# Seven block products in two more chunks of the first layer, and the last gate's conditioning beside a later stage

## The chip, the cores and the metric

One core of one Trainium2 chip runs the whole program. The metric is the device time of one execution in microseconds (us). The kernel before takes 2086.13 us, the median of three runs (2085.07 to 2087.54).

## The reference, cut to what matters

Two layers over 1024 prompt frames and 32 sample frames of width 1024. Each layer has a mixer and a channel MLP; the conditioning vector `mod` gives shifts, scales and gates. The change touches the MLP's second product and the conditioning.

```python
for i in range(DEPTH):                       # DEPTH = 2
    mod = silu(c) @ w_ada[i] + b_ada[i]      # w_ada[i]: 1024 x 6144
    sh1, sc1, gt1, sh2, sc2, gt2 = split(mod, 6)
    h = rmsnorm(x, g_norm[i, 0]) * (1 + sc1) + sh1
    mix = spatial gating MLP (layer 0) or pooling mixer (layer 1) of h
    x = x + gt1 * rmsnorm(mix, g_norm[i, 1])
    h = rmsnorm(x, g_norm[i, 2]) * (1 + sc2) + sh2
    f = square(relu(h @ ffn_w_up[i])) @ ffn_w_down[i]    # 1024 -> 4096 -> 1024
    x = x + gt2 * rmsnorm(f, g_norm[i, 3])
```

## The kernel before, in words

Activations lie transposed, channels on partitions and frames along the free axis, in three tiles: tiles 0 and 1 have 384 frames each (the pair), tile 2 has 256 prompt frames and the 32 sample frames. Every large product is made of three matmuls, because each operand is split into a high and a low part (`wh`, `wl` for weights, `hh`, `hl` or `fh`, `fl` for activations): wh·h, wh·l, wl·h. The high part is a copy by ScalarE, the low part a subtraction by VectorE.

The MLP runs in chunks of 512 of the 4096 hidden channels, in the order of the list `passes`: chunk 0 for tile 0 and for tile 1 alone, then chunks 1 to 7 for the pair (pair chunks), then four double chunks (0, 2, 4, 6) for tile 2 (the third-tile stage). A chunk has up products (`pf`, `pfa`, `pfb`, `pfc`) into PSUM, the squared ReLU, and down products (`pg`, or `psa`, `psb`, `psc`), which VectorE adds into the accumulator `acc`. In all pair chunks the up product of the two tiles by two halves of the contraction is a 2x2 block product done with seven block multiplications instead of eight (sums of blocks are made once, in `combos`). The down product does the same only in the chunks of the tuple `SEVEN`: there `sevens` makes weight sums for four parts A1, S31, S24, A22, `keep_seven` makes sums of the hidden blocks, and `down_seven` runs the products of `PLAN`. A plain down product of a pair chunk has 192 matmuls, one with seven block products 168. A chunk in `SEVEN` needs three more buffers, `far`, taken from the space of the third tile's accumulator, so whatever that tile still has to do must be finished first.

All weights and conditioning columns come in one list, `stream`, in program order, as loads of 512 KB into a ring of three buffers (`RAW_SLOTS = 3`, tile `raw`). A buffer is free again when ScalarE and VectorE have read it. Weights then go to ten to sixteen split buffers. A conditioning item (`wide`, tile `aa`) is 256 rows by 512 columns of `w_ada`: VectorE multiplies and adds it for both conditioning vectors, and after four items transposes, reduces and folds the sums. `some_ada(n)` puts n items at the current place of the stream; `w_chunk(n, ada)` puts one behind each up pair and each down weight until `ada` are used. The list `rest` ends with the eight items of the second layer's last gate (gt2 of layer 1).

While products are recorded, `weave` interleaves stream steps and `fillers` (norms, residuals, outputs) by a cost model of TensorE and VectorE; a scheduler then fixes one order per engine. SyncE issues nearly all loads and stores in its order. `to_out` is the filler that adds the last residual of tiles 0 and 1, transposes and stores the output; it calls `need_ada(1, 5)`, the last gate. `mix_to_ffn` prepares the third tile's input of the MLP; its last step waits in `late_norm` until the pair chunks are nearly through (`apply` in layer 0; in layer 1 a scaled copy goes to DRAM, and `shift` reads it back).

## Time and profile before

| | us |
|---|---|
| median of three runs | 2086.13 |
| profiled execution, its own time | 2085.84 |
| its span, first to last instruction | 2084.1 |
| TensorE busy | 2062.3 |
| VectorE busy | 1711.5 |
| ScalarE busy | 1114.4 |
| layer 0, pair chunk 5 / 6 / 7, start to start | 62.80 / 63.10 / 62.58 |
| layer 1, pair chunk 4 / 5 / 6 / 7 | 58.85 / 59.40 / 59.41 / 59.54 |
| layer 1, third tile, first / second double chunk | 53.77 / 51.01 |

A chunk is measured from its first up product to the next chunk's first up product, as the timeline of TensorE shows them. Busy time of an engine is the union of its instructions; matmuls overlap each other, so the time that one takes on the way is read from the distance of two starts and not from its length. An idle time is put down to the instruction whose semaphore came last.

### The profile page before, as it was taken

What the parts mean: (1) busy time and instruction counts of PE and PEld (TensorE: products, weight loads), DVE (VectorE), ACT (ScalarE), POOL (GpSimd) and SP (SyncE); (2) the same over time, 40 slices, a digit from 0 to 9 for tenths busy, and PEclk for the clock granted to TensorE, in tenths of its full rate; (3) what the DMA queues carried; (4) which work ended last, traced back from release to release, by engine and by line L of the source; (5) the groups of instructions that cost most, each with busy time, mean ns of one, the idle gap of its engine ahead of it and who ended that gap; (6) DMA issues with size and microseconds to landing.
All of it is one profiled execution on the core that took longest, in us unless ns stands there. A gap on an engine that the chain in (4) does not pass through costs nothing.

```text
span 2084.1 us, 33060 instructions
## 1 busy us (share of the span) xinstructions
PE 2062.3 (99%) x12646; PEld 1988.7 (95%) x12646; DVE 1711.5 (82%) x3149; ACT 1114.4 (53%) x2038; POOL 22.4 (1%) x44
## 2 busy tenths in 40 slices
PE   8999999999999999999999999999999999999998
PEld 5878999999999999999999999999999999999998
DVE  6799777889789998887877989897969688899644
ACT  5633543454247643344436766766445566685555
POOL 0000000000000000000000000000000000000200
PEclk9999999999999999999999999999999999999999
DMA  8585543366444343434334768553233222247873
GB/s 298 154 271 187 173 125 120 120 195 192 141 122 155 107 142 112 132 113 133 114 98 124 214 190 247 166 161 104 89 112 111 75 80 71 69 146 223 210 184 98
DMA packets 411923, 306.27 MB, mean 147 GB/s; under 512 B 47054, under 2 KB 375030, under 8 KB 411636
## 3 DMA queue, kind: packets, MB, share of 16 engines
q1 hardware_dynamic: 410836, 302.88, 47.5%
q8 instruction: 99, 1.62, 0.3%
q0 software_dynamic: 896, 1.28, 0.2%
q14 instruction: 60, 0.49, 0.1%
q10 hardware_dynamic: 32, 0.01, 0.0%
HBM read 272.27 MB, written 31.84 MB: 146 GB/s over the span
## 4 chain that ended last, share of the span: by engine, by line
PE 86%; DVE 7%; ACT 4%; DMA 2%; issue 1%; SPq 0%; DVEq 0%; ACTq 0%
PE pg L1174 9%; PE pg L1175 9%; PE pg L1176 9%; PE pf L1174 4%; PE pf L1176 4%; PE pf L1175 4%; PE pv L1200 2%; PE pv L1202 2%; PE pv L1201 2%; PE pfa L1852 2%; PE pfa L1854 2%; PE pfa L1853 2%; PE po L1174 2%; PE po L1175 2%; PE po L1176 2%; PE pu L1174 2%
## 5 line engine op out<-in xcount | busy, mean ns | idle before, releaser
L1174 PE MATMUL pg<-fh,wh_dn 128*128 128x384 f32 (+1 forms) x800 | 257.9, 323 | 1.4 <-ACT fh L1494 1.0
L1175 PE MATMUL pg<-fl,wh_dn 128*128 128x384 f32 (+1 forms) x800 | 256.7, 321 | 0.0
L1176 PE MATMUL pg<-fh,wl_dn 128*128 128x384 f32 (+1 forms) x800 | 256.4, 321 | 0.3 <-DVE wl_dn L80 0.3
L80 DVE SCALAR_TENSOR_TENSOR aa<-raw,csil,aa 128x512 f32<-128x512 f32 (+1 forms) x364 | 208.7, 623 | 8.3 <-DMA raw<-in_w_ada_dram 8.0
L1174 PE MATMUL pf<-hh,wh_up 128*128 128x288 f32 (+1 forms) x632 | 192.3, 304 | 0.0
L1175 PE MATMUL pf<-hl,wh_up 128*128 128x288 f32 (+1 forms) x632 | 191.1, 302 | 0.0
L1176 PE MATMUL pf<-hh,wl_up 128*128 128x288 f32 (+1 forms) x632 | 190.8, 302 | 0.0
L80 DVE TENSOR_TENSOR wl_dn<-raw,wh_dn 128x1024 fp32r<-128x1024 f32 x120 | 146.3, 1220 | 43.7 <-ACT wh_dn L629 31.4
L80 DVE TENSOR_TENSOR acc<-acc,pg 128x384 f32<-128x384 f32 (+1 forms) x208 | 108.7, 527 | 72.3 <-PE pg L1176 71.4
L629 ACT ACTIVATE wh_dn<-raw 128x1024 fp32r<-128x1024 f32 x120 | 126.9, 1058 | 71.1 <-PE pf L1175 31.3
L1174 PEld LDWEIGHTS pg<-fh,wh_dn 128*128 128x128 f32 x800 | 150.1, 188 | 2.9 <-ACT fh L1494 1.7
L1175 PEld LDWEIGHTS pg<-fl,wh_dn 128*128 128x128 f32 x800 | 150.2, 188 | 0.7 <-DVE fl L80 0.3
L1176 PEld LDWEIGHTS pg<-fh,wl_dn 128*128 128x128 f32 x800 | 150.1, 188 | 0.6 <-DVE wl_dn L80 0.6
L629 ACT ACTIVATE wh_up<-raw 128x1024 fp32r<-128x1024 f32 x79 | 83.6, 1058 | 74.9 <-PE pg L1175 43.8
L1176 PEld LDWEIGHTS pf<-hh,wl_up 128*128 128x128 f32 x632 | 118.9, 188 | 0.3 <-DVE wl_up L80 0.3
L1175 PEld LDWEIGHTS pf<-hl,wh_up 128*128 128x128 f32 x632 | 118.6, 188 | 0.5
L1174 PEld LDWEIGHTS pf<-hh,wh_up 128*128 128x128 f32 x632 | 118.4, 187 | 0.6 <-ACT wh_up L629 0.2
L80 DVE TENSOR_TENSOR wl_up<-raw,wh_up 128x1024 fp32r<-128x1024 f32 x79 | 96.2, 1220 | 18.7 <-ACT wh_up L629 18.7
L1174 PE MATMUL pg<-fx,wh_dn 128*128 128x288 f32 (+1 forms) x320 | 98.7, 309 | 0.1
L1175 PE MATMUL pg<-fx,wh_dn 128*128 128x288 f32 (+1 forms) x320 | 97.5, 305 | 0.0
L1176 PE MATMUL pg<-fx,wl_dn 128*128 128x288 f32 (+1 forms) x320 | 97.3, 304 | 0.0
L80 DVE TENSOR_TENSOR wl_up_S<-raw,wh_up_S 128x512 fp32r<-128x512 f32 (+1 forms) x84 | 71.6, 865 | 28.4 <-PE pfb L1853 16.2
(932 smaller groups left out, 6108.4 us busy)
## 6 DMA issues: line engine op xcount, KB each, us to landing
raw<-in_ffn_w_up_dram SPq DMA_DIRECT2D x136, 512.0 KB, 4.0
raw<-in_ffn_w_down_dram SPq DMA_DIRECT2D x136, 512.0 KB, 3.8
raw<-in_w_ada_dram SPq DMA_DIRECT2D x90, 512.0 KB, 4.1
raw<-in_sgu_w_in_dram SPq DMA_DIRECT2D x48, 512.0 KB, 4.3
raw<-in_sgu_w_out_dram SPq DMA_DIRECT2D x32, 512.0 KB, 3.6
xd<-acc SPq DMA_DIRECT2D x8, 1536.0 KB, 8.2
xo_r<-xd SPq DMA_DIRECT2D x32, 384.0 KB, 4.1
vd<-vt SPq DMA_DIRECT2D x32, 256.0 KB, 3.7
```

Of the source, the lines that this page charges most:

```text
L80: return op(out, *args, **kw)
L629: act(out=wh, in_=r, func=AF.Copy)
L1174: mm(ps[:, :n], wh, rh, start=i == 0, stop=False)
L1175: mm(ps[:, :n], wh, rl, start=False, stop=False)
L1176: mm(ps[:, :n], wl, rh, start=False, stop=i == last)
L1200: mm(ps[:m, :], a_h, wh[:, o : o + 512], start=k == 0, stop=False)
L1201: mm(ps[:m, :], a_h, wl[:, o : o + 512], start=False, stop=False)
L1202: mm(ps[:m, :], a_l, wh[:, o : o + 512], start=False, stop=k == KB - 1)
L1852: mm(ps[:, :n], wh[:, o], rh, start=first and k == 0, stop=False, skip_group_check=True)
L1853: mm(ps[:, :n], wh[:, o], rl, start=False, stop=False, skip_group_check=True)
L1854: mm(ps[:, :n], wl[:, o], rh, start=False, stop=k == HK - 1, skip_group_check=True)
```

## The change

Layer 0's pair chunks 5 and 6 join `SEVEN`. So that the third tile's accumulator is free for `far` there, layer 0's third tile takes the path that only layer 1 had: eight channel blocks are scaled in place, stored to a DRAM tile `scaled`, and read back by `shift`. In layer 1 the same copy now goes to `scaled` and not to `xd[2]`. Conditioning items move: layer 0's pair chunks had 5, 6, 6, 6, 6, 6, 1 (chunks 1 to 7) and now have 5, 7, 8, 8, 0, 0, 4; layer 1's pair chunks had the last four and now have none; the last gate's eight items stand in the first double chunk of layer 1's third tile. Within a chunk they are spread evenly over its calls. `to_out` waits until the stream has passed them. At the start of every down product with seven blocks, the first half of a third product is moved ahead.

```diff
+    scaled = dram.tile([P, KB, ncol[-1]], F32, name="scaled")
...
-        left = [ada]
+        at = [0]
         def one_ada():
-            if left[0] > 0:
-                left[0] -= 1
-                some_ada(1)
+            i, calls = at[0], 6 * m
+            at[0] += 1
+            some_ada((i + 1) * ada // calls - i * ada // calls)
...
-    SEVEN = ((1, 4), (1, 5), (1, 6), (1, 7))
+    SEVEN = ((0, 5), (0, 6), (1, 4), (1, 5), (1, 6), (1, 7))
...
-            w_chunk(n, (1 if c < 3 else 2) if l else (5 if c == 1 else 6) if c < 7 else 1)
+            w_chunk(n, 0 if l else {1: 5, 2: 7, 3: 8, 4: 8, 5: 0, 6: 0, 7: 4}[c])
             continue
-        w_chunk(n)
+        w_chunk(n, 8 if l and c == 0 and tiles == [NT - 1] else 0)
...
-            for i in (1, 5):
+            for i in (1, 5, 2):
                 product(0, i, (0,))
-            for i in (1, 5):
+            for i in (1, 5, 2):
                 product(0, i, (1,))
                 behind(0, i)
-            for i in (2, 6, 3, 7):
+            for i in (6, 3, 7):
                 run(0, i)
...
-            if l == 0:
-                late_norm.append((f"ffn{l}_{t}", apply(t, l, 2, 3, got[0])))
-                return
             for k in range(KB):                 # scale acc in place
...
-            nc.sync.dma_start(xd[t], acc[t][:, :, HALO:])
+            nc.sync.dma_start(scaled, acc[t][:, :, HALO:])
             late_norm.append((f"ffn{l}_{t}", shift(t, l)))
...
-        nc.sync.dma_start(hl[t].bitcast(F32), xd[t])
+        nc.sync.dma_start(hl[t].bitcast(F32), scaled)
...
+            while state["next"] <= max(ada_last[(1, 20 + i)] for i in range(4)):
+                yield 1.0
             need_ada(1, 5)
```

Three places of the built programs show the moves. First TensorE at the start of the down product of layer 0's chunk 5. In the names, `pg_5_0_0` is the accumulation of chunk 5, tile 0, first output block; `psa`, `psb`, `psc` are the three banks of the seven products, `fh` and `fl` hidden blocks split into high and low, B and T plain blocks and sums, `wh_dn_0_A` a weight part. Before:

```order
L1174 MATMUL pg_5_0_0_9905<-fh_5_0_0_9655,wh_dn_0_9766 128x384
L1175 MATMUL pg_5_0_0_9905<-fl_5_0_0_9656,wh_dn_0_9766 128x384
L1176 MATMUL pg_5_0_0_9905<-fh_5_0_0_9655,wl_dn_0_9767 128x384
L1174 MATMUL pg_5_0_0_9905<-fh_5_0_1_9685,wh_dn_0_9766 128x384
L1175 MATMUL pg_5_0_0_9905<-fl_5_0_1_9686,wh_dn_0_9766 128x384
```

The same place now:

```order
L1984 MATMUL psa_5_0_9963<-fh_5_B_0_9762,wh_dn_0_A_9796 128x384
L1985 MATMUL psa_5_0_9963<-fl_5_B_0_9763,wh_dn_0_A_9796 128x384
L1986 MATMUL psa_5_0_9963<-fh_5_B_0_9762,wh_dn_0_A_9796 128x384
L1984 MATMUL psb_5_0_9967<-fh_5_T_0_9767,wh_dn_0_S_9817 128x384
L1985 MATMUL psb_5_0_9967<-fl_5_T_0_9768,wh_dn_0_S_9817 128x384
L1986 MATMUL psb_5_0_9967<-fh_5_T_0_9767,wh_dn_0_S_9817 128x384
L1984 MATMUL psc_5_0_9971<-combo_R,wh_dn_0_A_9796 128x384
L1985 MATMUL psc_5_0_9971<-combo_R,wh_dn_0_A_9796 128x384
L1986 MATMUL psc_5_0_9971<-combo_R,wh_dn_0_A_9796 128x384
L1984 MATMUL psa_5_0_9963<-fx_5_B_1_9922,wh_dn_0_A_9796 128x384
L1985 MATMUL psa_5_0_9963<-fx_5_B_1_9922,wh_dn_0_A_9796 128x384
```

Seven products replace the plain ones, and the nine first matmuls use blocks of the first half; the late block `fx_5_B_1` comes tenth. Next VectorE in the first double chunk of layer 1's third tile, behind the last sums of the pair. `wl_up_4` is the low part of its fifth up weight, `aa_10` a conditioning sum, `acc_66` and `acc_67` are the accumulators of tiles 0 and 1, `sq_rf` their squares. Before:

```order
L80 TENSOR_TENSOR acc_66<-acc_66,da_7_3_19267 128x384
L80 TENSOR_TENSOR wl_up_4_19303<-raw_19173,wh_up_4_19302 128x1024
L80 TENSOR_TENSOR fl_0_2_0_19298<-r_0_2_0_19295,fh_0_2_0_19297 128x288
L80 TENSOR_TENSOR acc_67<-acc_67,psa_7_3_19184 128x384
L80 TENSOR_TENSOR wl_up_5_19316<-raw_19229,wh_up_5_19315 128x1024
L80 TENSOR_TENSOR sq_rf_0_19360<-sq_rf_0_19360 128x384
```

The same place now:

```order
L80 TENSOR_TENSOR acc_66<-acc_66,da_7_3_19360 128x384
L80 TENSOR_SCALAR aa_10_512_0_19363<-raw_19266,csil 128x512
L80 TENSOR_SCALAR aa_10_512_1_19364<-raw_19266,csil 128x512
L80 SCALAR_TENSOR_TENSOR aa_10_512_0_19363<-raw_19266,csil,aa_10_512_0_19363 128x512
L80 SCALAR_TENSOR_TENSOR aa_10_512_1_19364<-raw_19266,csil,aa_10_512_1_19364 128x512
L80 TENSOR_TENSOR fl_0_2_0_19399<-r_0_2_0_19396,fh_0_2_0_19398 128x288
L80 TENSOR_TENSOR wl_up_4_19404<-raw_19322,wh_up_4_19403 128x1024
L80 TENSOR_TENSOR acc_67<-acc_67,psa_7_3_19277 128x384
L80 TENSOR_TENSOR wl_up_5_19450<-raw_19352,wh_up_5_19449 128x1024
```

The conditioning stands in VectorE's row between the weights. From this sum up to and with the low part of the next double chunk's first weight, the row gains 40 instructions on `aa`, its transposes and reductions and one `xlast` transpose, and loses 14 of the output residual of tile 0. Last SyncE, some loads later in the same stage; before:

```order
L533 DMA raw_19409<-in_ffn_w_down_dram 128x8x128
L533 DMA raw_19454<-in_ffn_w_down_dram 128x8x128
L533 DMA raw_19503<-in_ffn_w_down_dram 128x8x128
L2086 DMA xraw<-xtd 32x32x32 x2
L533 DMA raw_19549<-in_ffn_w_down_dram 128x8x128
```

The same place now:

```order
L534 DMA raw_19673<-in_ffn_w_down_dram 128x8x128
L534 DMA raw_19716<-in_ffn_w_down_dram 128x8x128
L2087 DMA xraw<-xtd 32x32x32
L534 DMA raw_19778<-in_w_ada_dram 128x2x512
L534 DMA raw_19784<-in_ffn_w_down_dram 128x8x128
L534 DMA raw_19816<-in_w_ada_dram 128x2x512
L2087 DMA xraw<-xtd 32x32x32
```

Eight conditioning loads share the three `raw` buffers with the stage's sixteen weight loads. (`xraw` is the residual of the third tile for the end.)

## The prediction, as put on record before the change was run

> **What bounds the kernel now.** I read the page's busy shares first, then its chain of waits, then the windows chunk by chunk, then single rows of the timeline where a term needed them.
>
> ```profile
> span 2084.1 us, 33060 instructions
> PE 2062.3 (99%) x12646; PEld 1988.7 (95%) x12646; DVE 1711.5 (82%) x3149; ACT 1114.4 (53%) x2038; POOL 22.4 (1%) x44
> PE 86%; DVE 7%; ACT 4%; DMA 2%; issue 1%; SPq 0%; DVEq 0%; ACTq 0%
> ```
>
> TensorE is busy 99% of the span, and the chain runs over it for 86%. So a matmul less is a gain, and anything else counts only where it makes TensorE wait. The profiled execution took 2085.84 us: its span and 1.7 around it. The median of the runs is 0.3 higher; I sum against the former and add 0.3 at the end.
>
> Now the stages that the change touches, as windows between first up products. Columns: length, TensorE, its weight loads, VectorE, ScalarE, GpSimd, clock, DMA.
>
> ```profile
> core 0: us, PE busy (x) PEld busy (x) DVE busy (x) ACT busy (x) POOL busy (x), PEclk, DMA share, GB/s
> 757.06:820.55 63.49, 63.13 (x372) 62.78 (x372) 57.86 (x104) 26.86 (x48) 0.00 (x0) 1.00 0.38 117
> 820.55:883.45 62.90, 62.90 (x370) 62.62 (x369) 51.51 (x85) 26.94 (x47) 0.00 (x0) 1.00 0.37 118
> 883.45:945.85 62.40, 62.40 (x361) 62.40 (x361) 53.18 (x87) 24.93 (x45) 0.00 (x0) 1.00 0.38 119
> 945.85:1008.65 62.80, 62.80 (x369) 62.52 (x369) 50.34 (x81) 27.05 (x47) 0.00 (x0) 1.00 0.37 118
> 1008.65:1071.75 63.10, 62.97 (x370) 62.61 (x369) 52.69 (x87) 25.06 (x45) 0.00 (x0) 1.00 0.37 117
> 1071.75:1134.33 62.58, 62.58 (x361) 62.36 (x361) 43.30 (x77) 38.11 (x77) 0.00 (x0) 1.00 0.32 97
> 1628.61:1687.46 58.85, 58.48 (x332) 57.08 (x331) 49.47 (x97) 36.40 (x76) 0.00 (x0) 1.00 0.18 55
> 1687.46:1746.86 59.40, 59.25 (x338) 58.19 (x337) 52.78 (x103) 39.32 (x80) 0.00 (x0) 1.00 0.23 71
> 1865.81:1919.58 53.77, 53.42 (x395) 52.67 (x395) 50.19 (x81) 33.91 (x60) 1.28 (x2) 1.00 0.79 225
> 1919.58:1970.59 51.01, 51.01 (x387) 50.91 (x385) 37.01 (x54) 26.78 (x41) 13.61 (x22) 1.00 0.85 220
> ```
>
> The first six rows are layer 0's pair chunks 2 to 7 with the plain down product, the next two are layer 1's chunks 4 and 5 with seven block products, the last two are the first double chunks of layer 1's third tile. Everywhere TensorE has the full clock and almost no gap. VectorE has 5 to 20 us free in a pair chunk, but in the first double chunk of the third tile only 53.77 − 50.19 = 3.6.
>
> **Seven products in layer 0's chunks 5 and 6.** Each drops 24 of its 192 down matmuls. The trap is the matmul's length:
>
> ```profile
> 799.57 0.33 PE L1176 MATMUL pg<-combo_R,wl_dn 128*128 128x384 f32 x1
> 799.75 0.33 PE L1174 MATMUL pg<-fh,wh_dn 128*128 128x384 f32 x1
> 799.92 0.33 PE L1175 MATMUL pg<-fl,wh_dn 128*128 128x384 f32 x1
> 787.27:820.55 33.28, 33.28 (x192) 33.12 (x192) 8.21 (x15) 0.00 (x0) 1.00 0.44 132
> ```
>
> Each is listed at 0.33 us, but the next starts 0.17 later, and the last row, the window of one whole down product for its tile alone, gives 33.28 / 192 = 0.1733 us. So 48 matmuls are 8.3 us and not 15.8. The Trainium skill, "TensorE: Matmul & The Clock Gate", section "Wait — 56ns, not 53.3ns?", has a warm start-to-start of columns / 2.4 GHz + about 2.5 ns, an estimate of 0.1625 us for 384 columns; by it the 48 would save 7.8, and the trace's own 0.1733 decides.
>
> Not all of 8.3 arrives, since block sums and waits come with it. The windows say what does: chunks 5 and 6 take 62.80 + 63.10 = 125.90 now, and layer 1's chunks 4 and 5, the same two steps in the same order (first seven chunk, then one behind another), take 58.85 + 59.40 = 118.25. That is 7.65 less. But the last product of a seven chunk leaves its last six matmuls for the next chunk, so 6 × 0.1733 = 1.04 falls into chunk 7. **−6.6**. Ends: −8.3, no overhead at all; −6.0, if the first seven chunk also runs at 59.40. VectorE's 49.47 and 52.78 there hold norms that layer 0 has not at this place, and conditioning is moved out of both chunks, so nothing on VectorE should be fuller than in the template.
>
> **The third product's early half.** Seven down products now number six, and each opens with three more matmuls that need only first-half blocks.
>
> ```profile
> 1718.49 0.34 PE L1985 MATMUL psb<-fh_T,wh_dn_S 128*128 128x384 f32 x1
> 1718.98 0.44 PE L1983 MATMUL psa<-fx_B,wh_dn_A 128*128 128x384 f32 x1 [0.15 <-ACT fx_B L1494]
> 1719.42 0.55 DVE L80 TENSOR_TENSOR fx_B<-r,fx_B 128x384 fp32r<-128x384 f32 x1
> 1720.06 0.41 PE L1984 MATMUL psa<-fx_B,wh_dn_A 128*128 128x384 f32 x1
> ```
>
> Chunk 5 of layer 1: TensorE gets to the late block at 1718.98, waits for its high part, then for its low part, which VectorE ends at 1719.97; the next matmul is at 1720.06. Three matmuls (0.52) put in between push the block's first use back by about as much as they fill, and what follows starts about 0.1 earlier (1720.92 for 1721.01, by adding starts). 6 × 0.1 = **−0.6**; ends 0 and −3.0 (all of 0.5 each).
>
> **Conditioning in layer 0's chunks 1 to 4.** Chunks 2, 3, 4 get one, two and two more items, chunk 7 three more; the third tile's scaling (16 instructions) moves out of chunk 7 into this region, together with a store and a reload on SyncE's queue. The price of an item:
>
> ```profile
> 820.52 0.88 DVE L80 TENSOR_SCALAR aa<-raw,csil 128x512 f32<-128x512 f32 x2 [1.30 <-DMA raw<-in_w_ada_dram]
> 821.32 1.41 DVE L80 SCALAR_TENSOR_TENSOR aa<-raw,csil,aa 128x512 f32<-128x512 f32 x2
> 822.65 0.55 DVE L80 TENSOR_TENSOR acc<-acc,pg 128x384 f32<-128x384 f32 x1
> L80 DVE STREAM_TRANSPOSE raw<-aa 128x512 f32<-128x512 f32 x28 | 18.7, 692 | 0.0
> L733 DVE TENSOR_REDUCE part<-raw 128x16 f32<-128x512 f32 x28 | 18.1, 666 | 0.0
> ```
>
> Two multiply-adds take 1.33 from start to next start (0.665 each), two plain multiplies 0.80; each fold of four items has two transposes and two reductions, 18.7 / 28 = 0.67 and 18.1 / 28 = 0.65. An item is four passes, 2.66, and a quarter of a fold, some 3.1 us with its wait. Five items are 15.5, and 16 scalings at about 0.28 are 4.5 (estimate, from the 0.55 of a 384-column pass). Free in chunks 2 to 4 are 5.6, 11.4 and 9.2 us: 26.2 for 20. It fits, but the same row of VectorE also serves the sums that TensorE waits for, and chunk 2, the fullest of the three, shows 0.36 us of TensorE idle (63.49 − 63.13). Two such gaps: **+0.7**; ends 0 and +3 (one item's length, if one sum is late by a whole item). Chunk 7's three items, 9.3, lie in 62.58 − 43.30 = 19.3 free: 0. Cover gone, they would cost up to their length. The store and reload lie before chunk 5 in a queue at 0.38 DMA share: 0, unless `shift` is late for chunk 7's end, which is four chunks later.
>
> **Layer 1's chunks without items.** Four items leave chunks that had VectorE time free: **−0.2** (0 to −1).
>
> **The last gate in the third tile's first double chunk.** Here is the price. VectorE's row there, in rows from now:
>
> ```profile
> 1870.36 0.55 DVE L80 TENSOR_TENSOR acc<-acc,da 128x384 f32<-128x384 f32 x1
> 1885.26 0.40 PE L1176 MATMUL pg<-fh,wl_dn 128*128 128x288 f32 x1 [0.32 <-DVE wl_dn L80]
> 1890.10 1.23 DVE L80 TENSOR_TENSOR wl_dn<-raw,wh_dn 128x1024 fp32r<-128x1024 f32 x1 [1.41 <-ACT wh_dn L629]
> 1908.36 1.22 DVE L80 TENSOR_TENSOR wl_up<-raw,wh_up 128x1024 fp32r<-128x1024 f32 x1
> 1919.85 0.29 PE L1176 MATMUL pf<-hh,wl_up 128*128 128x288 f32 x1
> L80 DVE SCALAR_TENSOR_TENSOR acc<-acc,coef,r_rf 128x384 f32<-128x384 f32 x16 | 9.3, 610 | 0.0
> L80 DVE TENSOR_TENSOR acc<-acc,xo_r 128x768 f32<-128x768 f32 x8 | 7.6, 951 | 0.0
> L80 DVE STREAM_TRANSPOSE xlast<-xraw 128x1024 f32<-128x1024 f32 (+1 forms) x3 | 3.7, 1241 | 0.0
> ```
>
> Between the sum at 1870.36 and the next double chunk's first low part (1908.36, ready 1909.6, used first by the matmul at 1919.85) the row gains 28 × 0.665 + 4 × 0.40 + 4 × 0.67 + 4 × 0.65 = 25.5 and one transpose of 1.24, and loses 14 residual passes: 8 × 0.58, 3 × 0.95, 3 × 0.55 = 9.1. Net 17.6. The row is fixed, so the low part moves from 1909.6 to 1927.2, or to 1923.6 if all 3.6 of idle are filled. TensorE wants it at 1919.85: it waits 3.8 at least (3.0 if some of the passes overlap as starts do), 7.4 if no idle is filled.
>
> The loads can add to this. Sixteen weights and eight items share three buffers, where there were sixteen loads.
>
> ```profile
> raw<-in_ffn_w_up_dram SPq DMA_DIRECT2D x10, 512.0 KB, 4.7
> raw<-in_ffn_w_down_dram SPq DMA_DIRECT2D x8, 512.0 KB, 4.5
> raw<-in_w_ada_dram SPq DMA_DIRECT2D x90, 512.0 KB, 4.1
> L629 ACT ACTIVATE wh_up<-raw 128x1024 fp32r<-128x1024 f32 x9 | 9.5, 1057 | 8.4 <-PE pg L1175 7.2 <-DMA raw<-in_ffn_w_up_dram 1.2
> ```
>
> The first two are medians in this window, the third of the whole run. A buffer's turn is the landing, 4.6, and ScalarE's copy 1.06 and VectorE's subtraction 1.22, 6.9 us; for an item 4.1 and 2.66, 6.8. Twenty-four loads on three buffers are eight turns, 55 us if no turn waits for anything, as long as the stage. That reader passes queue behind each other's rows is sure, since VectorE would be full; with a wait of 1 us a turn, 63, which is 9.5 over 53.77. By slot and item, the twelve loads from the down weights to the next up weights run four turns of about 7.4, 30 us, where TensorE asks for eight weights at 3.2 (51.01 / 16), 25.6: 4 more. Part of that is the same delay as VectorE's. I take **+6** between +3.0 and +9.5, nearer to the row of VectorE, of which I am surer. The bytes themselves: 225 GB/s at a share of 0.79 make 285 at a full share; the stage's 12.1 MB and 4.2 more are 57.2 us by that, no more than VectorE's own floor.
>
> The Trainium skill, "DMA: Bandwidth & Descriptors", section "Anatomy of one DMA — SWDGE (gpsimd) path", gives a transfer 2.0 us and bytes / 436 GB/s, an estimate of 3.2 us for 512 KB. By it turns would be over 1 us shorter, VectorE alone would set the stage and the sum would be some 2 us lower. It is stated for GpSimd's path, and the rows of SyncE's queue, 4.1 to 4.7, disagree.
>
> Queued behind the items on SyncE are weights and `xraw`; behind them on VectorE the low parts, so TensorE. The residual and the stores of tiles 0 and 1 move later by about 50 us:
>
> ```profile
> L2489 SPq DMA_DIRECT2D out_dram<-y_sq x40: 316/562/1537, 1919.3 to 1999.2; - x40
> ```
>
> They would end near 2050, some 30 us before the span's end, and their passes fit the 14 us that VectorE has free in the second double chunk: 0.
>
> Sum: −6.6 − 0.6 + 0.7 − 0.2 + 6 = −0.7, own time 2085.1, with the 0.3 **2085.4**.
>
> **Rivals.** *The third tile's loss is small, faster.* If buffers turn in the shadow of VectorE and VectorE's passes overlap, the stage loses 3.0; with 0.3 in chunks 2 to 4 and 0.2 for each reordered start: −6.6 − 1.2 − 0.2 + 0.3 + 3.0 = −4.7, 2081.4. For it: the slack of 10 us between 1909.6 and 1919.85, in which a late low part hurts nobody. Against it: TensorE already waits 0.32 at 1885.26, in the middle of the stage, where no such slack exists.
>
> *The ring bounds the stage, slower.* If every one of eight turns waits 1.35 (about VectorE's one idle of 1.41 for a copy, or one low part ahead), the stage takes 8 × 8.25 = 66, +12.2; with −6.7 elsewhere, +5.5: 2091.6. It decides from a loss of 10.9 in the stage on. For it: DMA share 0.79 and landings longer here than elsewhere. Against it: loads run ahead of the stage, and the pair chunks before it leave the ring idle most of the time.
>
> *Seven chunks save less in layer 0 than in layer 1*, because chunk 4's eight items reach into chunk 5, where VectorE makes 24 hidden sums: both chunks at about 60.9 instead of 59.1 lose some 3 us: 2088.4. Against it: nothing of conditioning is due in chunks 5 and 6.
>
> **How the numbers follow.** Differences under 0.2% (4.2 us) can't be told from none, so faster is below 2082.0 and slower above 2090.3. Forecast 0.42, small loss 0.30, ring 0.18, dearer seven chunks 0.10, of which 0.06 within the bound. Faster 0.30, same 0.48, slower 0.22. The range goes from 2079.5 (small loss with the early halves at −3) to 2091.5 (the ring's case), leaving out about one in ten on each side.
>
> **What would show it.** Right: chunks 5 and 6 of layer 0 at about 58.9 and 59.4; chunks 2 to 4 each within 0.7 of now; the third tile's first double chunk at 57 to 63, TensorE waiting there for `wl_dn` and `wl_up`, VectorE for `raw`; last stores of tiles 0 and 1 before 2060. Wrong: that stage under 56 or over 64, a seven chunk over 60.5, or waits that move into the second double chunk, where the residual's passes would then stand in the way.

## The result: 2108.05 us, 1.0% slower

The changed kernel takes 2108.05 us, the median of four runs (2105.77 to 2110.45), against 2086.05 for the kernel before on the same chip; the ratio is 1.0105, with a 95% interval of 1.0087 to 1.0122. The forecast was 2085.4, in a range of 2079.5 to 2091.5. The profiled execution took 2109.03, its span 2107.2.

From the page of the changed kernel, the lines that answer to those shown of before, and the group of the conditioning sums:

```profile
span 2107.2 us, 33152 instructions
PE 2063.9 (98%) x12598; PEld 1984.4 (94%) x12598; DVE 1749.4 (83%) x3247; ACT 1139.9 (54%) x2106; POOL 22.4 (1%) x44
PE 77%; DVE 11%; DMA 5%; ACT 5%; issue 2%; DVEq 0%; ACTq 0%; SPq 0%
L80 DVE SCALAR_TENSOR_TENSOR aa<-raw,csil,aa 128x512 f32<-128x512 f32 (+1 forms) x364 | 206.8, 621 | 16.6 <-DMA raw<-in_w_ada_dram 16.4
```

TensorE has 48 matmuls less and 23 us more span. The chain of waits tells where: TensorE's share fell from 86% to 77%, VectorE's rose from 7% to 11% and that of the transfers from 2% to 5%. VectorE waits 16.4 us in front of conditioning sums for their loads, 8.0 before, with the same number of sums.

Windows of the changed kernel, columns as before: layer 0's chunks 3, 4, 5, 6; its chunk 7 together with the third tile's first double chunk; layer 1's chunk 7 together with the third tile's first double chunk; the second double chunk. Chunk 7 and what follows are taken together because a few matmuls of the third tile now run ahead inside chunk 7.

```profile
core 0: us, PE busy (x) PEld busy (x) DVE busy (x) ACT busy (x) POOL busy (x), PEclk, DMA share, GB/s
819.03:885.64 66.61, 64.48 (x369) 62.42 (x369) 57.31 (x95) 25.68 (x46) 0.00 (x0) 1.00 0.40 126
885.64:952.19 66.55, 64.56 (x370) 62.32 (x370) 56.14 (x90) 25.67 (x46) 0.00 (x0) 1.00 0.41 128
952.19:1010.49 58.30, 57.85 (x331) 57.18 (x331) 50.25 (x98) 38.10 (x78) 0.00 (x0) 1.00 0.24 72
1010.49:1069.87 59.38, 58.88 (x337) 58.24 (x337) 52.76 (x103) 39.36 (x80) 0.00 (x0) 1.00 0.23 71
1069.87:1191.59 121.72, 118.79 (x765) 117.19 (x765) 106.64 (x176) 80.91 (x150) 0.00 (x0) 0.99 0.58 176
1813.22:1935.39 122.17, 114.88 (x728) 111.84 (x727) 108.91 (x195) 78.55 (x161) 0.00 (x0) 0.99 0.54 159
1935.39:1992.15 56.76, 54.68 (x397) 53.42 (x398) 48.26 (x77) 29.11 (x47) 4.36 (x7) 0.97 0.75 210
```

The same two joined stages before:

```profile
1071.75:1186.50 114.75, 114.75 (x751) 114.32 (x751) 92.05 (x149) 78.52 (x147) 0.00 (x0) 1.00 0.49 147
1806.27:1919.58 113.31, 112.81 (x731) 110.89 (x731) 103.30 (x190) 82.49 (x167) 1.28 (x2) 1.00 0.56 164
```

By start-to-start distances the whole difference is laid out:

| stage | before | changed | difference | forecast |
|---|---|---|---|---|
| up to layer 0's chunk 2 | 757.06 | 755.17 | −1.9 | 0 |
| layer 0, chunks 2, 3, 4 | 188.8 | 197.0 | +8.2 | +0.7 |
| layer 0, chunks 5, 6 | 125.9 | 117.7 | −8.2 | −7.6, less starts |
| layer 0, chunk 7 and third tile's first double chunk | 114.8 | 121.7 | +7.0 | +1.0 |
| rest of layer 0's third tile, layer 1 up to its pair chunks | 228.5 | 231.4 | +2.9 | 0 |
| layer 1, chunks 1 to 6 | 391.3 | 390.2 | −1.1 | −0.2, less starts |
| layer 1, chunk 7 and third tile's first double chunk | 113.3 | 122.2 | +8.9 | +6 |
| layer 1, third tile, the rest to the last matmul | 157.5 | 164.9 | +7.4 | 0 |

The gain came as forecast. Four stages gave back 31.5 us, nearly four times as much. In the rows that were read, TensorE waits there for a split weight or a hidden block that comes late from VectorE or ScalarE; its two longest waits in the third tile's first double chunk of layer 1 are these (us in total, times, longest):

```profile
PE pg L1177 <- DVE wl_dn L80: 3.5, 3, 2.1
PE pg L1175 <- ACT wh_dn L630: 2.6, 2, 1.4
```

Of the −1.9 ahead of chunk 2, 1.1 lies in chunk 1, whose five items stand one call later than before: 78.2 for 79.3. Place matters in this direction too.

### The profile page after: what moved, and what is told of

It reads as the page before. It is cut to its first block, busy times and chain, and to the rows that moved or that the text cites. A ratio compares the mean times of both kernels' runs of the same rounds, so it can differ in the third digit from the quotient of the medians.

```text
span 2107.2 us, 33152 instructions
## 1 busy us (share of the span) xinstructions
PE 2063.9 (98%) x12598; PEld 1984.4 (94%) x12598; DVE 1749.4 (83%) x3247; ACT 1139.9 (54%) x2106; POOL 22.4 (1%) x44
## 4 chain that ended last, share of the span: by engine, by line
PE 77%; DVE 11%; DMA 5%; ACT 5%; issue 2%; DVEq 0%; ACTq 0%; SPq 0%
PE pg L1175 7%; PE pg L1176 7%; PE pg L1177 7%; PE pf L1177 3%; PE pf L1175 3%; PE pf L1176 3%; PE pv L1201 2%; PE pv L1203 2%; PE pv L1202 2%; PE pfa L1853 2%; PE pfa L1855 2%; PE pfa L1854 2%; DMA raw<-in_w_ada_dram 2%; PE po L1176 2%; PE po L1175 2%
## 5 line engine op out<-in xcount | busy, mean ns | idle before, releaser
L1175 PE MATMUL pg<-fh,wh_dn 128*128 128x384 f32 (+1 forms) x720 | 231.8, 322 | 4.4 <-ACT wh_dn L630 2.6
L1177 PE MATMUL pg<-fh,wl_dn 128*128 128x384 f32 (+1 forms) x720 | 230.5, 320 | 3.6 <-DVE wl_dn L80 3.5
L1176 PE MATMUL pg<-fl,wh_dn 128*128 128x384 f32 (+1 forms) x720 | 230.6, 320 | 2.4 <-DVE fl L80 2.4
L80 DVE SCALAR_TENSOR_TENSOR aa<-raw,csil,aa 128x512 f32<-128x512 f32 (+1 forms) x364 | 206.8, 621 | 16.6 <-DMA raw<-in_w_ada_dram 16.4
L80 DVE TENSOR_TENSOR wl_dn<-raw,wh_dn 128x1024 fp32r<-128x1024 f32 x112 | 136.2, 1219 | 28.8 <-ACT wh_dn L630 19.9
L630 ACT ACTIVATE wh_dn<-raw 128x1024 fp32r<-128x1024 f32 x112 | 118.2, 1057 | 71.9 <-DMA raw<-in_ffn_w_down_dram 41.8
L1175 PEld LDWEIGHTS pg<-fh,wh_dn 128*128 128x128 f32 x720 | 135.5, 188 | 6.8 <-ACT wh_dn L630 3.4
L1177 PEld LDWEIGHTS pg<-fh,wl_dn 128*128 128x128 f32 x720 | 135.5, 188 | 4.5 <-DVE wl_dn L80 4.5
L1176 PEld LDWEIGHTS pg<-fl,wh_dn 128*128 128x128 f32 x720 | 135.6, 188 | 3.1 <-DVE fl L80 2.9
L80 DVE TENSOR_TENSOR acc<-acc,pg 128x384 f32<-128x384 f32 (+1 forms) x176 | 91.5, 522 | 50.3 <-PE pg L1177 49.6
L1175 PE MATMUL pg<-fx,wh_dn 128*128 128x288 f32 (+1 forms) x304 | 93.3, 308 | 1.6 <-ACT fx L1495 1.6
L1176 PE MATMUL pg<-fx,wh_dn 128*128 128x288 f32 (+1 forms) x304 | 91.9, 303 | 0.0
```

Source lines behind the costliest of these rows:

```text
L80: return op(out, *args, **kw)
L630: act(out=wh, in_=r, func=AF.Copy)
L1175: mm(ps[:, :n], wh, rh, start=i == 0, stop=False)
L1176: mm(ps[:, :n], wh, rl, start=False, stop=False)
L1177: mm(ps[:, :n], wl, rh, start=False, stop=i == last)
```

## The experiments

Most edits change only where conditioning items stand and which chunks are in `SEVEN`. `w_chunk` gets the number of items for each of its six calls in a pair chunk (behind two up pairs, then four down weights) as a list:

```diff
-            some_ada((i + 1) * ada // calls - i * ada // calls)
+            some_ada(ada[i] if ada else 0)
```

A reader needs the changed kernel's lists: chunk 2 has 1,1,1,1,1,2, chunks 3 and 4 have 1,1,2,1,1,2, chunk 7 has 0,1,1,0,1,1, and the third tile's double chunk 0,1,1,0,1,1,0,1,1,0,1,1. "Joined" means chunk 7 with the double chunk behind it. The kernel before, measured beside the experiments, took 2086.57 us (e1 to e4), 2087.61 (e5 to e8), 2088.24 (e9 to e13, one run) and 2087.64 (e14, e15), and each total below is to be held against its own.

**e1: the last gate's items in layer 1's pair chunks.**

```diff
-(1, 1), (1, 2), (1, 3): no items; third tile: 8
+(1, 1): [0,0,1,0,0,1], (1, 2): [0,1,0,1,0,1], (1, 3): [0,1,0,1,0,1]; third tile: none
```

> The changed kernel with one thing moved: the last gate's eight items stand in layer 1's pair chunks 1, 2, 3 (two, three, three) and not in the third tile's first double chunk. Theory P (the items in the third-tile stage are the price there: 62.40 and 56.70 us in the first two double chunks for 53.77 and 51.01 before, and 2 at the end): those windows go back to within 1 us of before, a gain of 14 to 16; layer 1's chunks 1 to 3 show 10 to 20 us of free VectorE time each and lose 0 to 3; time about 2094 (2092 to 2097). Rival Q (an item costs what it costs wherever it stands, since VectorE is late everywhere in pair chunks too): chunks 1 to 3 of layer 1 grow by some 1 us an item, 8 together; time about 2100.

Measured: 2109.07 us, ratio 1.0110 (1.0093 to 1.0127), no better than the change.

```profile
1572.48:1644.63 72.15, 67.79 (x388) 66.03 (x388) 56.98 (x106) 33.66 (x62) 0.00 (x0) 0.99 0.37 108
1644.63:1709.62 64.99, 62.09 (x333) 59.47 (x333) 50.75 (x110) 37.08 (x78) 0.00 (x0) 0.96 0.25 76
1829.02:1942.50 113.48, 112.44 (x731) 110.92 (x731) 103.63 (x190) 82.37 (x167) 1.28 (x2) 1.00 0.56 164
1942.50:1993.51 51.01, 51.01 (x387) 50.91 (x385) 36.57 (x54) 26.78 (x41) 13.57 (x22) 1.00 0.84 218
```

The last two rows are back at 113.3 and 51.0, so the first half of theory P is shown. But chunks 3 and 4 of layer 1 (first two rows) went from 62.95 and 58.54 to 72.15 and 64.99. Some 14 us moved along with the items (chunks 1 to 6 together). With 15 us of VectorE free in the 72.15 window, that is not plain lack of time. Part of it is this: the first seven block chunk (4) takes the third tile's accumulator, so that tile's norm must be finished by then, and TensorE stood 3.7 us for it just ahead of chunk 4. Rival Q had the direction, and 8 was too little.

**e2: the items' loads without most of their passes.**

```diff
+                if l == 1 and sl >= 10 and (c, v) != (0, 0) and not (q == 0 and c == 0):
+                    continue
```

> The changed kernel, but the last gate's eight items keep all eight loads and their places in the ring, and leave out 22 of their 32 VectorE passes (so the last gate is not computed fully). Theory V (VectorE's row is the bound of the third tile's first double chunk): 22 x 0.665 = 14.6 us less on VectorE, the window goes from 62.40 to 54 to 56. Rival R (the ring of three buffers with 24 loads is the bound): the window stays at 60 or more, and TensorE and VectorE still wait for wh and raw.

Measured: 2105.32 us (one run). Joined stage 119.39 for 122.17, second double chunk 52.28 for 56.76. Taking out 22 passes, 14.6 us by their length, won 7.3 (VectorE's busy time in the two windows fell by 11.7). Neither theory holds alone; TensorE still waited 5.7 us at one place for a `wh_dn` that was loaded late.

**e3: other calls, same numbers.**

```diff
-(0, 3): [1,1,2,1,1,2], (0, 4): [1,1,2,1,1,2], (0, 7): [0,1,1,0,1,1]
+(0, 3): [2,2,1,1,1,1], (0, 4): [1,1,1,1,2,2], (0, 7): [2,2,0,0,0,0]
```

> The changed kernel with the same number of items in each chunk of layer 0, at other calls: chunk 3 has 2,2,1,1,1,1 (two up pairs, four down weights) for 1,1,2,1,1,2; chunk 4 has 1,1,1,1,2,2; chunk 7 has its four behind the two up pairs, 2,2,0,0,0,0, for 0,1,1,0,1,1. Theory S (the loss is a matter of place: the double item at the first down weight, and in chunk 7 an item whose load comes late, stand in VectorE's row ahead of the hidden blocks that the down product starts on): chunk 3 or 4 falls from 66.6 to 63 to 64, chunk 7 from 70.6 to about 65. Rival N (the number of items fills VectorE, whatever the place): chunks 3 and 4 stay within 1 us of 66.6, chunk 7 of 70.6.

Measured: 2105.66 us (one run). Chunk 3 fell from 66.6 to 64.18, chunk 4, with its doubles at the end, rose to 68.87, the joined chunk 7 fell from 121.7 to 119.47. Place is worth some 2 us a chunk in either direction, number the other half: nothing came back to 62.4 or 114.8. Rows of the changed kernel show the place. VectorE, then TensorE, in chunk 4:

```profile
909.38 5.39 DVE L80 SCALAR_TENSOR_TENSOR aa<-raw,csil,aa 128x512 f32<-128x512 f32 x8
920.15 0.87 DVE L80 TENSOR_SCALAR aa<-raw,csil 128x512 f32<-128x512 f32 x2
920.94 1.41 DVE L80 SCALAR_TENSOR_TENSOR aa<-raw,csil,aa 128x512 f32<-128x512 f32 x2
922.26 1.02 DVE L80 TENSOR_TENSOR combo_R<-r,combo_R 128x384 fp32r<-128x384 f32 x2
921.99 0.86 PE L1175 MATMUL pg<-combo_R,wh_dn 128*128 128x384 f32 x3 [1.11 <-ACT combo_R L1495]
```

and in chunk 7:

```profile
1099.47 1.42 DVE L80 SCALAR_TENSOR_TENSOR aa<-raw,csil,aa 128x512 f32<-128x512 f32 x2 [3.58 <-DMA raw<-in_w_ada_dram]
1100.80 0.56 DVE L80 TENSOR_TENSOR r<-a,b 128x384 f32<-128x384 f32 x1
1103.07 0.55 DVE L80 TENSOR_TENSOR fl<-r,fh 128x384 fp32r<-128x384 f32 x1
1103.67 0.44 PE L1176 MATMUL pg<-fl,wh_dn 128*128 128x384 f32 x1 [1.94 <-DVE fl L80]
1105.27 0.69 PE L1176 MATMUL pg<-combo_R,wh_dn 128*128 128x384 f32 x1 [0.81 <-DVE combo_R L80]
```

The double item puts eight passes in a row (5.4 us) between VectorE's last hidden blocks. In chunk 7 VectorE does nothing for 3.58 us: it stands before an item whose load is late, and the sum `r` behind it, from which the down product's hidden block is made, stands too.

**e4: plain down products, items as in the change.**

```diff
-    SEVEN = ((0, 5), (0, 6), (1, 4), (1, 5), (1, 6), (1, 7))
+    SEVEN = ((1, 4), (1, 5), (1, 6), (1, 7))
```

> The changed kernel with layer 0's chunks 5 and 6 on the plain down product again, all conditioning items where the changed kernel has them. If seven block products alone gave the 8.2 us that chunks 5 and 6 show: they take 62.5 each here (192 + 168 matmuls at 0.1733 us) for 58.3 and 59.4, some 7 us more together, chunk 7 loses the six carried matmuls, 1.0; own time about 2108 + 6 = 2114. If chunks 5 and 6 are shorter mostly because they have no items (rival): at most 3 us longer here, time 2110.

Measured: 2113.55 us (one run). Chunks 5 and 6 took 62.67 and 62.77, so seven block products are worth 7.8 there, items or not. The joined chunk 7 fell to 117.22: a chunk behind a seven block chunk is 4.5 dearer, of which the carried matmuls are 1.0.

**e5: seven block products in layer 0's last pair chunk only.** Layer 1's four items are where they were before.

```diff
+    SEVEN = ((0, 7), (1, 4), (1, 5), (1, 6), (1, 7))
+(0, 1): [1,1,1,1,1,0], (0, 2) to (0, 5): 6 each, (0, 6): [2,1,1,1,1,1], (0, 7): none
+(1, 1), (1, 2): [1,0,0,0,0,0], (1, 3): [1,1,0,0,0,0]; third tile: none
```

> Seven block products in layer 0 only in chunk 7, the last pair chunk: the one conditioning item that stood there goes to chunk 6 (seven items, the double one behind the first up pair), layer 1 keeps its four items in chunks 1 to 3 at the first calls, the third-tile stage gets none. Theory A (the seven block products pay what the windows of chunks 5 and 6 showed, and the loss of the change is the items' new places): chunk 7 and layer 0's third tile together fall from 114.75 to about 112, layer 1's chunk 7 and third tile stay at 113.3 and 51.0, chunk 6 grows by at most 1; time 2083 to 2085, 1 to 3 below before. Rival B (a seven block chunk in layer 0 loses its gain in what follows it, as chunk 7 behind chunk 6 lost 7): the two together stay at 114 to 117, time 2086 to 2089.

Measured: 2091.39 us, ratio 1.0018 (1.0009 to 1.0027). Theory A fails on the total. The joined stage is 114.50, nothing won, and the two double chunks after it took 121.9 for 116.7 before, with waits of 1.0 us for `wh_dn` and 1.4 for a norm. Rival B holds in kind, and the loss was larger than it said.

**e6: the residual of tiles 0 and 1 postponed, without items in the way.** The kernel of e5, and

```diff
-            while state["next"] <= max(ada_last[(1, 20 + i)] for i in range(4)):
+            while state["next"] <= out_mark[0]:
```

where `out_mark` is the place of the first double chunk's last down weight in the stream.

> The kernel of e5 with one thing changed: the output residual of tiles 0 and 1 (to_out) waits until the stream has passed the last down weight of the third tile's first double chunk in layer 1, as in the changed kernel, but no conditioning item stands there. Theory P (the items' passes and loads are the price of the first two double chunks): the first double chunk stays at 51 to 54 with chunk 7 before it, the second at 51 to 52, the end within 1 us; time within 2 us of e5. Rival O (the postponed residual is a good part of the price): the second double chunk takes 54 to 57 as in the changed kernel, the last 56 to 58; time 4 to 8 above e5.

Measured: 2087.15 us (one run); the joined stage 113.92, the second double chunk 50.99. The postponed residual and its stores cost nothing by themselves, where no items stand beside them. (The 4 us to e5 lie in layer 0's third tile, ahead of the edit: 53.61 for 56.61 in its second double chunk; one run of each doesn't tell whether this is chance.)

**e7: seven block products in chunk 6 only.**

```diff
+    SEVEN = ((0, 6), (1, 4), (1, 5), (1, 6), (1, 7))
+(0, 2), (0, 3), (0, 4): [2,1,1,1,1,1], (0, 5): 6, (0, 6): none, (0, 7): [2,2,0,0,0,0]; layer 1 as in e5
```

> Seven block products in layer 0 only in chunk 6: items 5, 7, 7, 7, 6, 0, 4 in chunks 1 to 7, doubles behind the first up pair, chunk 7's four behind the two up pairs; layer 1 keeps its four, the third-tile stage gets none. Theory A: chunk 6 saves 4.8 (58.3 for 63.1), three seventh items cost 0.4 to 1 each, chunk 7 with the third tile's stage costs 1.0 of carried matmuls and 1 to 3 for the four items: time 2083 to 2087. Rival B (four items in chunk 7 behind a seven block chunk cost the 7 us of the changed kernel wherever they stand): time 2088 to 2092.

Measured: 2093.2 us, ratio 1.0024 (1.0014 to 1.0034): rival B. Chunk 6 saved 4.6 (58.49). The joined chunk 7 took 120.39, 5.6 over before, and chunk 3 alone 67.75 with seven items, while chunks 2 and 4 took 63.7 and 62.8 with the same seven, within 0.4 of before.

**e8: earlier calls in layer 0, half of the gate in layer 1's pair chunks.**

```diff
+(0, 2): [2,1,1,1,1,1], (0, 3), (0, 4): [2,2,1,1,1,1], (0, 7): [2,2,0,0,0,0]; (1, 1) to (1, 3) as in e5
+third tile: [0,0,1,0,0,1,0,0,1,0,0,1]
```

> The changed kernel (seven block products in layer 0's chunks 5 and 6) with the doubles of chunks 2, 3, 4 behind the up pairs, chunk 7's four items behind the two up pairs, four of the last gate's items back in layer 1's chunks 1 to 3 at the first calls and four, not eight, in the third tile's first double chunk. Theory S and P: chunks 3 and 4 at 64 to 65 for 66.6, chunk 7 with layer 0's third tile 2 less, the third-tile stage of layer 1 loses about half of the 16: time 2092 to 2096. Rival: the price of the third-tile stage doesn't go with the number of items (the wait for the residual and the ring is there with four too): time 2098 or more.

Measured: 2099.66 us (one run). Chunks 3 and 4 took 64.62 and 64.96, the joined chunk 7 120.62, layer 1's joined stage 116.50 and the second double chunk 51.67. In those two, four items cost 3.9 where eight cost 14.6. But the last double chunk, to the end, grew from 55.27 to 60.96 (57.24 in the changed kernel): TensorE waits 2.40 us there for `wh_up`, and why that weight is late was not traced. Over the whole third tile half the items thus cost 9.2 of 16.3, more than half the price, and the time is the rival's.

**e9: four and four in the first two double chunks.**

```diff
-third tile: {0: 8}
+third tile: {0: 4, 2: 4}, each [0,0,1,0,0,1,0,0,1,0,0,1]
```

> The changed kernel with the last gate's eight items split over the first two double chunks of layer 1's third tile, four and four, and not all eight in the first. The windows read are layer 1's chunk 7 with the first double chunk (113.31 before, 122.16 changed), the second (51.01, 56.76), the third (51.18, 50.87), the last to the end (55.27, 57.24). Theory F (VectorE and the ring are full only together: four items fit into the free VectorE time and the free turns of a double chunk, and what stands above that makes TensorE wait one for one): 116.5 and 53 to 54, 10 less in the first two, time about 2099. Rival L (each item costs 1.8 us wherever it stands in the third tile): the same 15 over the two stages, 117.5 and 58, time 2106 to 2108.

Measured: 2106.43 us (one run). Joined 116.95, then 50.97, 57.07 and 56.8 to the end: 11.0 over before in all, 16.3 in the changed kernel. The second four cost 5.9, in the window after the one they were put into; why more than the first four, with 3.6, was not traced. Against the changed kernel the first two stages got 11.0 shorter, as F had it, but the third got 6.2 longer, which F had not; the time is near L's figure. Neither holds whole.

**e10: chunk 7 without items, old start order.**

```diff
-(0, 1): [0,1,1,1,1,1], (0, 7): [0,1,1,0,1,1]; for i in (1, 5, 2), then (6, 3, 7)
+(0, 1): [2,2,1,1,1,2], (0, 7): none; for i in (1, 5), then (2, 6, 3, 7)
```

> The changed kernel with layer 0's chunk 7 free of conditioning: its four items stand in chunk 1 (nine there), and the down products with seven blocks start in the old order (the third product's first half not moved ahead). Chunk 7 with layer 0's third tile up to its second double chunk was 114.75 before and 121.72 changed. Theory C (the four items' passes and late loads at the start of the down product cost the 7, beyond the 1.0 of six carried matmuls): 116 here. Rival K (a chunk behind a seven block chunk is late by its weights, whatever stands in it): 119 or more. Old start order: if moving the third product's half ahead gave what the prediction said (0.1 a product), chunks 5, 6 of layer 0 and 4 to 7 of layer 1 are each within 0.3 of the changed kernel's; if it gave 0.5 each, they are 0.5 longer. Chunk 1 grows by some 5 to 12.

Measured: 2131.08 us (one run).

```profile
757.62:829.44 71.82, 65.42 (x371) 62.56 (x371) 60.15 (x106) 26.00 (x48) 0.00 (x0) 1.00 0.42 130
829.44:903.95 74.51, 67.16 (x369) 63.51 (x369) 61.73 (x102) 25.48 (x46) 0.00 (x0) 0.98 0.39 120
903.95:974.15 70.20, 65.35 (x369) 62.27 (x369) 57.48 (x92) 25.37 (x46) 0.00 (x0) 1.00 0.39 120
1097.78:1215.44 117.66, 116.47 (x758) 115.29 (x757) 95.07 (x154) 80.63 (x150) 0.00 (x0) 1.00 0.54 162
```

The last row is the joined chunk 7: 117.66, so seven block products ahead of it cost 2.9 by themselves (1.0 carried), the four items 2.5 by themselves (e4), and both 7.0 (a backlog of 1.0 in chunk 6 may have reached chunk 7 here, so 2.9 is an upper bound). The first three rows are chunks 2, 3 and 4: four more items in chunk 1 cost chunks 1 to 6 together 27 us, about 6.8 an item, though these windows show 12 to 13 us without VectorE work. Layer 1's chunks 4 to 6 in the old start order took 58.50, 59.41 and 59.40, in the new 58.54, 59.38 and 59.35: the reordered start gives nothing.

**e12: half the loads, all passes.**

```diff
+        if l == 1 and sl >= 10 and q % 2:
+            ada_last[(l, 2 * sl)] = ada_last[(l, 2 * sl + 1)] = len(stream) - 1
+            return
...
+            if key[0] == 1 and key[1] >= 10:
+                do_ada(key[0], key[1], key[2] + 1, r, 512)
```

> The changed kernel with four of the eight loads of the last gate left out: every second item is computed from the load of the one before it (so the last gate's values are others), all 32 passes, transposes and reductions on VectorE stay. Run e2 kept the eight loads and left 22 passes out, and won back 2.8 in chunk 7 with the first double chunk and 4.5 in the second. If the ring's turns are the other half of the price: 119 or less in the first and 54 or less in the second. If VectorE's passes alone are the price and e2 was held up by something else: 121 to 123 and 56 to 57 as in the changed kernel.

Measured: 2109.65 us (one run); joined 127.07, second double chunk 51.15. Inconclusive: the eight passes of a pair stand in one piece, and TensorE waited 3.8 us for the fold of the sums, a wait that the changed kernel hasn't at this size.

**e13: the conditioning's move alone.**

```diff
+    SEVEN = ((1, 4), (1, 5), (1, 6), (1, 7))
+(0, 1): [1,1,1,1,1,0], (0, 2) to (0, 5): 6 each, (0, 6): [1,1,1,0,0,0], (0, 7): none; third tile: 8
```

> The conditioning's move alone: plain down products in all pair chunks of layer 0, items 5, 6, 6, 6, 6, 3, 0 in its chunks 1 to 7, none in layer 1's pair chunks, the last gate's eight in the third tile's first double chunk as in the changed kernel. If the third-tile stage's price stands by itself: layer 0 within 2 us of before, layer 1's last stages 14 to 17 longer, time 2100 to 2104. If part of it comes from what layer 0's seven block chunks do to the state in which the stage is entered: less than 10 longer, time below 2097.

Measured: 2104.7 us (one run), a little above the expected band, and 16.5 over the kernel before beside it.

```profile
821.67:884.57 62.90, 62.90 (x369) 62.62 (x369) 51.93 (x86) 27.25 (x47) 0.00 (x0) 1.00 0.39 118
884.57:946.98 62.41, 62.41 (x362) 62.41 (x362) 51.75 (x84) 24.92 (x45) 0.00 (x0) 1.00 0.39 119
1073.87:1188.71 114.84, 114.84 (x752) 114.29 (x751) 91.75 (x149) 77.63 (x146) 0.00 (x0) 1.00 0.51 157
1807.67:1931.99 124.32, 116.34 (x728) 113.13 (x727) 108.38 (x194) 78.22 (x160) 0.00 (x0) 0.97 0.54 157
1931.99:1987.26 55.27, 53.06 (x398) 51.80 (x397) 48.56 (x78) 29.04 (x46) 3.73 (x6) 1.00 0.76 214
```

With six items a chunk and the third tile's scaling, store and reload in place, layer 0's chunks 3 and 4 and the joined chunk 7 take what they took before (chunk 2 took 0.7 more, chunk 6 1.0). The last two rows carry 15.3 of the loss, the last double chunk 2.7 more. So the third-tile stage's price stands by itself, and in layer 0 it is the seventh and eighth item that cost, not the scaled path.

**e14: six of the eight loads outside the ring.** They go to the room of tiles 1 and 0's inputs (`h`), which is free after chunk 7's up products.

```diff
-        return kind != "x" and not (kind == "ada" and k < first_ada)
+        return kind != "x" and not (kind == "ada" and k < first_ada) and own(k) is None
...
+            elif own(k) is not None:
+                t, j = divmod(own(k), 3)
+                t = 1 - t
+                if t not in own_room:
+                    own_room[t] = room("h", t, f"own{t}").rearrange("p k n -> p (k n)")
+                r = own_room[t][:, 1024 * j : 1024 * j + 1024]
```

> The changed kernel, but six of the last gate's eight loads go to buffers of their own (the room of tiles 0 and 1's inputs, free once their last up product has run) and take no turn of the three-buffer ring; every VectorE pass stays, and so does the place of the items in the stream. Windows: layer 1's chunk 7 with the first double chunk 113.31 before and 122.16 changed, the second 51.01 and 56.76, the last 55.27 and 57.24. If the ring's turns are a good part of the price: 115 to 119 and 51 to 53, time 2098 to 2103. If VectorE's passes in its fixed row set it: 121 to 123 and 55 to 57, time 2106 to 2110.

Measured: 2101.82 us (one run).

```profile
1813.88:1930.25 116.37, 112.34 (x728) 110.21 (x727) 108.42 (x195) 78.26 (x161) 0.00 (x0) 1.00 0.57 168
1930.25:1985.08 54.83, 53.17 (x396) 51.91 (x397) 48.21 (x77) 29.14 (x47) 3.73 (x6) 1.00 0.76 215
```

VectorE does the same work (108.42 for 108.91) and the joined stage is 5.8 shorter, the second double chunk 1.9. So of the 14.6 lost in the two, at least 7.7 are the ring's turns.

What is left, 3.1 and 3.8, is not all VectorE's row. The six loads now go out between 1838 and 1852, beside the read of `scaled`, and in chunk 7 a wait stands that the changed kernel doesn't have: ScalarE waits for that read, and TensorE for the weight behind it.

```profile
1851.82 1.33 ACT L2185 ACTIVATE hh<-hl,mod 128x256 fp32r<-128x256 f32 x4 [1.38 <-DMA hl<-scaled]
1853.72 0.44 PE L1999 MATMUL psa<-fh_B,wh_dn_A 128*128 128x384 f32 x1 [1.42 <-ACT wh_dn_A L610]
```

VectorE's row can be read by itself, from the last sum of tile 0 to the next double chunk's first low part, as the prediction did. The changed kernel first, then this one:

```profile
1877.73 0.55 DVE L80 TENSOR_TENSOR acc<-acc,da 128x384 f32<-128x384 f32 x1
1936.40 1.22 DVE L80 TENSOR_TENSOR wl_up<-raw,wh_up 128x1024 fp32r<-128x1024 f32 x1
1879.74 0.55 DVE L80 TENSOR_TENSOR acc<-acc,da 128x384 f32<-128x384 f32 x1
1931.23 1.21 DVE L80 TENSOR_TENSOR wl_up<-raw,wh_up 128x1024 fp32r<-128x1024 f32 x1
```

From start to start that is 58.7 and 51.5, where the kernel before has 38.0 (1870.36 to 1908.36). So the row grew by 13.5 with most turns of the ring gone, and by 20.7 with them. In the changed kernel SyncE's waits in this stage were

```profile
SPq L534 <- DVE aa L80: 15.4, 6, 4.3
SPq L534 <- DVE wl_dn L80: 12.9, 7, 3.2
```

(columns: us, times, longest). The first was not there before: a weight's load stands behind an item's sums. In e14 the wait for `aa` is 2.2, once, and that for `wl_dn` 18.6.

**e15: the best of these together.** e14's buffers, the items four and four, layer 0's calls as in e8.

```diff
+(0, 2): [2,1,1,1,1,1], (0, 3), (0, 4): [2,2,1,1,1,1], (0, 7): [2,2,0,0,0,0]; third tile: {0: 4, 2: 4}
```

> As e14, with the last gate's items split four and four over the first two double chunks (the first six loads in buffers of their own) and layer 0's items at the early calls as in e8 (chunks 3 and 4 at 64.6 and 65.0 there, 4.6 us won in layer 0 over the changed kernel). Split items cost 3.6 and 5.9 in e9 with the ring; if the ring is a good part of that, 2 and 2 here: time about 2094. If VectorE sets it, as in e9: time about 2101.

Measured: 2097.16 us, ratio 1.0053 (1.0036 to 1.0070). Joined 115.88, then 51.01, 53.19: 2.6 and 2.0 over before for four items each, as the ring's part of the theory said; layer 0's chunks 2 to 4 and 7 keep the rest. No version tried with seven block products in layer 0 is clearly faster than the kernel before; e6, one run, is level with it.

## Why the prediction was wrong, step by step

**Seven block products: right.** Forecast −7.65 in chunks 5 and 6 by the template of layer 1, measured −8.2 (7.8 of it by e4, where the items are away too); the 1.0 carried into chunk 7 is in the windows (e4, e10).

**The reordered start: mis-sized, −0.6 forecast, 0 measured** (e10). It lay inside its bounds.

**Conditioning in chunks 2 to 4: the term that failed by most for its size, +0.7 forecast, +8.2 measured, outside its own end of +3.** The step of the prediction that failed reads "Free in chunks 2 to 4 are 5.6, 11.4 and 9.2 us: 26.2 for 20. It fits". Free time of a window is not free time where the pass stands. What ended VectorE's idle time in chunk 4 of the kernel before (us, times, longest):

```profile
DVE wl_up_S L80 <- PE pfb L1853: 3.5, 1, 3.5
DVE aa L80 <- DMA raw<-in_w_ada_dram: 2.3, 2, 1.9
DVE acc L80 <- PE pg L1176: 1.7, 2, 1.5
DVE fl L80 <- ACT fh L1494: 1.2, 1, 1.2
```

Over chunks 2, 3 and 4, 12.6 us of it end with a product of TensorE, 5.4 with a copy by ScalarE, and 8.6 with the load of a conditioning item: a third of the "free" time was conditioning waiting for its own loads. An item can use idle time only if it stands in the row just there and its load has landed. In e13 these chunks have six items each, as before, and the scaling, and take +0.7; so +0.7 is the scaling's price alone (that it equals the forecast is luck), and the five added items cost the other 7.5. Their price goes with place as well as with number: in e7 a seventh item cost 0.2 and 0.4 in chunks 2 and 4 and 4.9 in chunk 3.

**Chunk 7's three items at 0: failed, +5.9 beyond the carried matmuls.** "9.3 lie in 62.58 − 43.30 = 19.3 free" is the same step. The sentence behind it, that without cover they would cost up to their length, held. Seven block products ahead make it worse (2.5 and 1.9 alone, 5.9 together): a guess that isn't tested further is that their weights hold the ring through four steps each, so that chunk 7's items come late.

**The last gate in the third tile: the two causes were right, the place of the wait and the size not.** For the first double chunk +6 was forecast between 3.0 and 9.5, and 8.9 came. VectorE's row was counted well: 17.6 longer was forecast, 14.0 if all idle is filled, and e14 shows 13.5. The ring was too small a term: its turns cost at least 5.8 here, and the row grew by 20.7. The forecast let TensorE wait at the next double chunk's first `wl_up`; it waits before that, inside the stage, for `wl_dn` and `wh_dn` (6.1 together). And the sum ended there: the second double chunk lost 5.8 and the last ones 1.6, where the prediction had only the residual, at 0. The residual by itself is indeed 0 (e6). In the second double chunk TensorE waits 1.0 for `fx`, 0.6 for `part` (the fold of the last items) and 0.4 for `wl_up`, spends 1.1 on twelve small matmuls that were not in this window before, and runs a stretch at half speed, 1.4 (last section); the other 1.2 was not traced.

**The rivals.** "The ring bounds the stage" named half of the mechanism, with a loss of 12.2 in the first double chunk where 8.9 came, but its time of 2091.6 rested on −6.7 for all the rest, and the rest was +14. "Seven chunks save less" put chunks 5 and 6 at 60.9, and they took 58.30 and 59.38; "small" had 3.0 for the stage. The forecast held three terms, each "fits", as independent small numbers; they shared one assumption, that free time can be used wherever it lies, and all three fell short. Even all three at their worst ends, +3, +9.3 and +9.5, would have given 2100.5: the first end was too near, and the stages behind the overfull one were left out.

Of the 2.9 us in the rest of layer 0's third tile and the way to layer 1's pair chunks, 1.3 is one wait of TensorE for `wh_up` from ScalarE, at 1389.08, in layer 1. The whole 2.9 goes with the two seven block chunks: with none or with chunk 6 alone (e4, e13, e7) this stretch is within 0.4 of before, and with chunks 5 and 6 together it is 2.7 to 4.0 longer in every run. How they cause it stays open.

## What to carry to other kernels

Before work is moved to an engine with idle time, look at what ended that idle time: idle that waits for another engine's result is room only for work that stands just there in its row with its inputs landed; a share of 80 to 90% can be full. Passes that hold a shared ring buffer cost twice, once on their engine and once as later loads for everyone else; give such loads buffers of their own where space has just come free (at least 7.7 of 14.6 us here), and look what their earlier issue then holds up (1.4 in e14). And price the stage behind an overfull one too: backlog is handed on, 6.8 us for an item of 3.1 in e10.

## What the runs showed of the hardware

A wait can cost more than its length. TensorE in the changed kernel, behind a wait of 2.06 us in layer 1's third tile (start, duration):

```profile
1895.91 0.40 PE L1177 MATMUL pg<-fh,wl_dn 128*128 128x288 f32 x1 [2.06 <-DVE wl_dn L80]
1896.15 0.29 PE L1175 MATMUL pg<-fh,wh_dn 128*128 128x288 f32 x1
1896.28 0.29 PE L1176 MATMUL pg<-fl,wh_dn 128*128 128x288 f32 x1
...
1897.24 0.44 PE L1175 MATMUL pf<-hh,wh_up 128*128 128x288 f32 x1
1897.48 0.44 PE L1176 MATMUL pf<-hl,wh_up 128*128 128x288 f32 x1
```

It starts again at one matmul every 0.13 us, and 1.3 us after the restart drops to one every 0.24 us, for 13 matmuls: 1.4 us on top of 2.06. The same came in chunk 7 behind waits of 1.94 and 0.81 (nine matmuls of 384 columns at 0.32 and not 0.17, 1.3 us), and at the start of the second double chunk (1.4): some 4 of the 22 us. Over the whole run the mean granted clock is 0.996 for 0.998 before. The length of one wait doesn't decide it: the second double chunk began with waits of 0.54 and 0.63 only, and the waits of 1.1 us in chunks 3 and 4 and one of 1.44 for `wh_dn` showed none. The Trainium skill, "TensorE: Matmul & The Clock Gate", section "HAM oscillation — how this bites in real kernels", warns of idle gaps above about 3.4 us and half the clock behind them; half the clock agrees with these rows (0.24 for 0.13), and the gap was shorter here.
